# A kernel of two transformer layers whose Fourier stage is computed over half of the frequencies, two groups at a time

## The chip, the cores and the metric

The kernel runs on one core of a Trainium2 chip. The metric is the device time of one execution in microseconds (us): the median over runs, 1680.04 us for the kernel before (three runs, 1679.36 to 1681.76). All inputs, weights included, lie in the chip's main memory at the start.

## The reference, cut to what matters

The model has two layers. Each has a token mixer and a channel mixer, both with a modulated norm ahead and a residual add behind, on 256 tokens of context and 256 tokens of x, each 1024 wide. Half of the mixer's width (512) goes through a gated linear attention, the other half through a Fourier mix:

```
def fourier_mix(u):
    B, L, _ = u.shape                                   # L = 256
    ug = u.reshape(B, L, FNET_GROUPS, FNET_GROUP_DIM)   # 4 groups of 128
    y = jnp.fft.fftn(ug, axes=(1, 3), norm='ortho').real
    return y.reshape(B, L, FNET_WIDTH)

mx = jnp.concatenate([fourier_mix(ux), yx], axis=-1) @ w_out   # yx: the attention
x = x + g1x * mx
hx = modulate(rmsnorm(x, norm_ffn_w[l]), sh2x, sc2x)
x = x + g2x * channel_mixer(hx, ...)     # layer 0: SwiGLU; layer 1: 8 experts
```

The context takes the same path in layer 0; the last layer computes only x behind its attention. The gates and shifts (g1x, sh2x, ...) are sums of a vector of 1024 with a matrix `w_mod` of 1024 x 6144 for each layer.

## The kernel before, in words

Every product of fp32 matrices is made of three matmuls in a rounded format: each operand x is split into a high part (ACT copies x into the rounded type, line 145 for weights) and a low part (DVE subtracts the high part from x, line 149), and `mm3` (lines 155 to 158) adds high x high (L156), low x high (L157) and high x low (L158) in one PSUM bank. A split of one operand is thus one ACT and one DVE instruction, and the first matmul waits for ACT, the one that takes the low part for DVE.

The Fourier mix (`fourier`, lines 729 to 758) takes one sequence of 256 tokens and one group of 128 channels at a time: eight pairs of both in layer 0, four in layer 1. Stage 1 transforms along the tokens: two `mm3` (two blocks of 128 tokens) with the split table `dl_h`, `dl_l` of 512 columns, 256 cosines and 256 sines; ACT and DVE split the result into `vh` and `vl` (L752, L753). Stage 2 (`along_group`) transforms along the channels of a group: two `mm3` with the tables `dd_h`, `dd_l` on the cosine half and the sine half of `vh`, `vl`, both added in one bank of 256 columns; ACT and DVE split this into a block of `cat` (L740, L741), which is an operand of the output projection. Stage 2 of a group is issued behind stage 1 of the next.

Around it: the attention (`gla`), of which pieces are pulled in between groups; `w_out` (the output projection, lines 812 to 860), two halves of 512 columns for each sequence, with its weights split in L145 and L149 and the results multiplied and added to the residual by DVE (L829, L830); and the modulation sums of `mod_chunk`: DVE multiplies and adds blocks of `w_mod` (L422, 128x512 each), PE sums the 128 partitions of the result by four matmuls of one column (L432), DVE copies the sums (L434) into `modc`, and `ac` (L356) is made of `modc`. The norm ahead of the channel mixer (`Norms`, `h_steps`) squares the residual on ACT (L934), takes the root (L195), scales on DVE (L947, `xn`), transposes `xn` on PE (L290, 16 for a sequence), and makes from each transposed block, by `ac` and `modc`, the value (L303 on ACT or L301 on DVE), its high part (L304 or L300, ACT) and its low part (L305, DVE) in `hbk`. The feed-forward of layer 0 begins with three products on the context's tokens alone (72 matmuls of 256 columns), then takes the transposes and blocks of x, then three products on x alone; from there it takes all 512 tokens at once.

The order of the instructions on each engine is fixed when the program is built: a scheduler places each instruction by its priority (its place in the program text, changed by `high_priority` and by `later` for L422) and by its own estimate of when its inputs are ready. So a change of durations in one place can move other instructions past each other.

## Time and profile before

| | |
|---|---|
| median of three runs | 1680.04 us |
| the profiled execution, its own time | 1679.86 us |
| its span, first to last instruction | 1678.1 us |
| PE (TensorE matmuls) busy | 97% of the span |
| DVE (VectorE) busy | 63% |
| ACT (ScalarE) busy | 43% |
| mean granted TensorE clock | 0.993 of full speed |
| Fourier stage of layer 0 | about 179 to 216 us |
| output projection of layer 0 | about 213 to 262 us |
| feed-forward of layer 0 | from 263 us |
| Fourier stage of layer 1 | about 745 to 763 us |
| experts | about 800 to 1660 us |

A matmul is shown with the time that it takes through the array, and matmuls overlap; what one costs is the distance from its start to the next one's. An idle time of PE stands in square brackets, with what ended it. In the rows by windows the columns are the window, its length, then busy us of PE, weight loads, DVE, ACT and POOL with the number of instructions, the granted clock, the busy share of the DMA engines and the GB/s that they moved. In the rows by lines the columns behind the bar are the busy time in us, the mean ns of one, and the idle time ahead of them with what ended it.

### The profile page before, as it was taken

What the parts mean: (1) busy time and instruction counts of PE and PEld (TensorE: products, weight loads), DVE (VectorE), ACT (ScalarE), POOL (GpSimd) and SP (SyncE); (2) the same over time, 40 slices, a digit from 0 to 9 for tenths busy, and PEclk for the clock granted to TensorE, in tenths of its full rate; (3) what the DMA queues carried; (4) which work ended last, traced back from release to release, by engine and by line L of the source; (5) the groups of instructions that cost most, each with busy time, mean ns of one, the idle gap of its engine ahead of it and who ended that gap; (6) DMA issues with size and microseconds to landing.
All of it is one profiled execution on the core that took longest, in us unless ns stands there. A gap on an engine that the chain in (4) does not pass through costs nothing.

```text
span 1678.1 us, 21544 instructions
## 1 busy us (share of the span) xinstructions
PE 1620.3 (97%) x8134; PEld 1168.2 (70%) x8134; DVE 1049.4 (63%) x1318; ACT 726.0 (43%) x890; POOL 26.9 (2%) x51
## 2 busy tenths in 40 slices
PE   7999999999999999999999999999999999999995
PEld 3777888788888888788787347874468844578532
DVE  3798898778667657756996217862078820588322
ACT  3733445322222246554775126751167611567201
POOL 1000000000000000000000000000000000000000
PEclk9999999999999999999999999999999999999998
DMA  9524375556666534545898999999999999999995
GB/s 362 164 85 131 113 250 167 153 180 184 189 198 191 155 126 137 177 164 196 323 359 314 400 408 413 407 411 407 408 411 411 409 390 408 410 414 406 387 405 199
DMA packets 186795, 479.01 MB, mean 285 GB/s; under 512 B 11761, under 2 KB 65201, under 8 KB 172081
## 3 DMA queue, kind: packets, MB, share of 16 engines
q1 hardware_dynamic: 185040, 473.80, 76.4%
q10 hardware_dynamic: 1074, 2.72, 0.5%
q8 instruction: 68, 1.11, 0.3%
q0 software_dynamic: 560, 0.94, 0.2%
q14 instruction: 53, 0.43, 0.1%
HBM read 476.37 MB, written 1.05 MB: 285 GB/s over the span
## 4 chain that ended last, share of the span: by engine, by line
PE 87%; DVE 5%; DMA 3%; ACT 2%; issue 1%; SPq 0%; POOL 0%; DVEq 0%; ACTq 0%; POOLq 0%
PE h L1582 11%; PE mm L156 9%; PE mm L157 9%; PE mm L158 8%; PE h L1591 6%; PE h L1594 6%; PE h L1590 6%; PE y L156 5%; PE y L157 5%; PE y L158 5%; PE y L1614 4%; DMA rr<-moe_w 2%; PE sc L589 1%; PE sc L1561 1%; PE sc L1383 1%
## 5 line engine op out<-in xcount | busy, mean ns | idle before, releaser
L145 ACT ACTIVATE hi<-raw 128x1024 fp32r<-128x1024 f32 x127 | 134.5, 1060 | 309.2 <-PE mm L157 94.2
L177 DVE TENSOR_TENSOR rb<-raw,rb 128x2048 fp32r<-128x2048 f32 x73 | 167.1, 2290 | 79.8 <-ACT rb L177 59.6
L149 DVE TENSOR_TENSOR lo<-raw,hi 128x1024 fp32r<-128x1024 f32 x127 | 155.3, 1224 | 87.6 <-ACT hi L145 86.3
L422 DVE SCALAR_TENSOR_TENSOR rr<-rr,cs,rr 128x512 f32<-128x512 f32 x256 | 181.7, 748 | 10.9 <-DMA rr<-b_mod 5.3
L1591 PE MATMUL h<-rb,hg 128*128 128x512 f32 x448 | 177.2, 395 | 4.1 <-DVE rb L177 4.0
L156 PE MATMUL mm<-hbk,hi 128*128 128x512 f32 (+1 forms) x456 | 166.5, 366 | 0.9 <-DVE tm L829 0.7
L157 PE MATMUL mm<-hbk,hi 128*128 128x512 f32 (+1 forms) x456 | 163.7, 360 | 0.5 <-DVE hbk L305 0.5
L158 PE MATMUL mm<-hbk,lo 128*128 128x512 f32 (+1 forms) x456 | 163.7, 359 | 0.0
L177 ACT ACTIVATE rb<-raw 128x2048 fp32r<-128x2048 f32 x73 | 139.9, 1917 | 50.7 <-PE h L1594 31.9
L1582 PE MATMUL h<-raw,hgs 128*64 128x512 f32 (+1 forms) x720 | 143.4, 529 | 0.0
L177 DVE TENSOR_TENSOR sil<-sil,h 128x512 f32<-128x512 f32 (+1 forms) x44 | 29.2, 663 | 165.7 <-PE h L1582 148.5
L1590 PE MATMUL h<-rb,hg 128*128 128x512 f32 x288 | 109.1, 399 | 1.6 <-ACT rb L177 1.6
L1582 PEld LDWEIGHTS h<-raw,hgs 128*64 128x64 f32 x720 | 51.6, 137 | 77.5 <-issue 68.9
L1591 PEld LDWEIGHTS h<-rb,hg 128*128 128x128 f32 x448 | 85.2, 190 | 26.1 <-DVE rb L177 6.3
L177 DVE TENSOR_TENSOR rb<-raw,part 128x2048 fp32r<-128x2048 f32 x42 | 96.1, 2288 | 10.5 <-PE h L1591 4.6
L156 PEld LDWEIGHTS mm<-hbk,hi 128*128 128x128 f32 x456 | 85.8, 189 | 16.3 <-issue 2.4
L177 DVE TENSOR_TENSOR rb<-rr,rb 128x2048 fp32r<-128x2048 f32 x35 | 80.0, 2288 | 27.2 <-ACT rb L177 23.7
L177 ACT ACTIVATE part<-raw 128x2048 fp32r<-128x2048 f32 x42 | 80.4, 1914 | 36.4 <-DMA raw<-moe_w 17.0
L157 PEld LDWEIGHTS mm<-hbk,hi 128*128 128x128 f32 x456 | 85.9, 189 | 14.1 <-issue 1.0
L158 PEld LDWEIGHTS mm<-hbk,lo 128*128 128x128 f32 x456 | 85.9, 189 | 13.0
L1594 PE MATMUL h<-rb,hg 128*128 128x512 f32 x288 | 88.5, 393 | 2.5 <-DVE hg L177 2.5
L157 PE MATMUL y<-rb,ht 128*128 128x512 f32 x224 | 87.6, 391 | 0.0
(381 smaller groups left out, 2984.6 us busy)
## 6 DMA issues: line engine op xcount, KB each, us to landing
raw<-moe_w SPq DMA_DIRECT2D x212, 1024.0 KB
rr<-moe_w SPq DMA_DIRECT2D x110, 1024.0 KB
rr<-w_mod SPq DMA_DIRECT2D x80, 512.0 KB
raw<-ffn_w SPq DMA_DIRECT2D x72, 512.0 KB
raw<-w_in SPq DMA_DIRECT2D x32, 512.0 KB
raw<-w_out SPq DMA_DIRECT2D x23, 512.0 KB
raw<-moe_w SPq DMA_DIRECT2D x12, 512.0 KB
rb<-w_mod SPq DMA_DIRECT2D x5, 1024.0 KB
```

Of the source, the lines that this page charges most:

```text
L145: ins = nc.scalar.activation(hi, raw, AF.Copy).ins
L149: nc.vector.tensor_tensor(lo, raw, hi.bitcast(F32), op=OP.subtract)
L156: nc.tensor.matmul(ps, lh, rh, start=start, stop=False)
L157: nc.tensor.matmul(ps, lh, rl, start=False, stop=False)
L158: nc.tensor.matmul(ps, ll, rh, start=False, stop=stop)
L177: r = getattr(self.engine, name)(*args, **kw)
L422: nc.vector.scalar_tensor_tensor(accs[x], rv[:, k, :], cs[:, x * 8 + kb:x * 8 + kb + 1], accs[x], op0=OP.mult, op1=OP.add)
L1582: nc.tensor.matmul(H[i][0][x * 64:x * 64 + 64, :n], HG[e][:, k0 + j, :], hi[:, j, x * n:(x + 1) * n], start=(k0 + j == 0), stop=(k0 + j == 7))
L1590: nc.tensor.matmul(H[i][b], hgh[:, kb, :], hi[:, j, bc], start=(kb == 0), stop=False)
L1591: nc.tensor.matmul(H[i][b], hgh[:, kb, :], lo[:, j, bc], start=False, stop=False)
L1594: nc.tensor.matmul(H[i][b], hgl[:, kb, :], hi[:, j, bc], start=False, stop=(kb == 7))
L1614: nc.tensor.matmul(Y[e][0][hh * 64:hh * 64 + 64], ht[:, j0 + j, half], hi[:, j, xc], start=on, stop=off)
```

## The change

The token transform of a real sequence has a symmetry: cosines of frequency l and 256 - l are the same, sines differ in sign. So the table keeps 128 cosine columns (frequencies 0 to 127), the cosine of frequency 128 in the unused place of sine 0, and 127 sine columns. Stage 1 takes 256 columns for a group instead of 512, and the bank of 512 holds two groups, so that one ACT and one DVE instruction split both; the tiles of the table (`dlr`, `dl_h`, `dl_l`) and its load are half as wide. In stage 2 the cosine part and the sine part of two groups are products of 256 columns of their own (no sum of both on PE), the frequency 128 is a `mm3` of four columns into another bank (`mid`), ACT copies the sine part to SBUF (`sn`), DVE adds both parts for the frequencies 1 to 127 and subtracts them, written backwards, for 255 to 129, ACT copies two single columns for 0 and 128, and from this `y`, in SBUF now, ACT and DVE make the high and low part of each group, as before from PSUM. Stage 2 of two groups is issued behind stage 1 of the next two.

```diff
-    dl = np.concatenate([np.cos(ang), np.sin(ang)], 1).reshape(2, 128, 512).transpose(1, 0, 2)
+    dl = np.concatenate([np.cos(ang[:, :128]), np.cos(ang[:, 128:129]), np.sin(ang[:, 1:128])], 1)
+    dl = dl.reshape(2, 128, 256).transpose(1, 0, 2)
...
-            def along_group(s, g, vh, vl):
-                p2 = psp.tile([128, 512], F32, name="mm", tag="mm", bufs=4)[:, :256]
+            def along_groups(s, g, vh, vl):
+                bank_ = psp.tile([128, 512], F32, name="mm", tag="mm", bufs=4)
+                p2 = bank_.rearrange("p (c g l) -> p c g l", c=2, g=2)
                 for r in range(2):
-                    rr = slice(r * 256, (r + 1) * 256)
-                    mm3(p2, dd_h[:, r, :], dd_l[:, r, :], vh[:, rr], vl[:, rr], r == 0, r == 1)
-                cb = cat(g)
+                    mm3(p2[:, r].rearrange("p g l -> p (g l)"), dd_h[:, r, :], dd_l[:, r, :],
+                        vh[:, r].rearrange("p g l -> p (g l)"), vl[:, r].rearrange("p g l -> p (g l)"), True, True)
+
+                mid = bank()[:, 0:4].rearrange("p (g l) -> p g l", g=2)
+                mm3(mid, dd_h[:, 0, :], dd_l[:, 0, :], vh[:, 1, :, 0:2], vl[:, 1, :, 0:2], True, True)
+                sn = temp()[:, 0:256].rearrange("p (g l) -> p g l", g=2)
+                nc.scalar.activation(sn.rearrange("p g l -> p (g l)"), bank_[:, 256:512], AF.Copy)
+                y = temp().rearrange("p (g l) -> p g l", g=2)
+                nc.vector.tensor_tensor(y[:, :, 1:128], p2[:, 0, :, 1:128], sn[:, :, 1:128], op=OP.add)
...
+                nc.vector.tensor_tensor(back, p2[:, 0, :, 1:128], sn[:, :, 1:128], op=OP.subtract)
+                nc.scalar.activation(y[:, :, 0:1], p2[:, 0, :, 0:1], AF.Copy)
+                nc.scalar.activation(y[:, :, 128:129], mid[:, :, 0:1], AF.Copy)
                 o0 = s * 256 - coff
-                hi, lo = cb[:, 0, o0:o0 + 256], cb[:, 1, o0:o0 + 256]
-                nc.scalar.activation(hi, p2, AF.Copy)
-                nc.vector.tensor_tensor(lo, p2, hi.bitcast(F32), op=OP.subtract)
+                for k in range(2):
+                    cb = cat(g + k)
+                    hi, lo = cb[:, 0, o0:o0 + 256], cb[:, 1, o0:o0 + 256]
+                    nc.scalar.activation(hi, y[:, k], AF.Copy)
+                    nc.vector.tensor_tensor(lo, y[:, k], hi.bitcast(F32), op=OP.subtract)
 
             for s in seqs:
-                for g in range(4):
-                    vh = mx.tile([128, 512], F32R, name="vh", tag="vh", bufs=2)
-                    vl = mx.tile([128, 512], F32R, name="vl", tag="vl", bufs=2)
+                for g in (0, 2):
+                    vh = mx.tile([128, 2, 2, 128], F32R, name="vh", tag="vh", bufs=2)
+                    vl = mx.tile([128, 2, 2, 128], F32R, name="vl", tag="vl", bufs=2)
                     ps = psp.tile([128, 512], F32, name="mm", tag="mm", bufs=4)
-                    for t in range(2):
-                        uc = slice(g * 128, (g + 1) * 128)
-                        mm3(ps, uh[:, 2 * (s - sb) + t, uc], ul[:, 2 * (s - sb) + t, uc], dl_h[:, t, :], dl_l[:, t, :],
-                            t == 0, t == 1)
-                    nc.scalar.activation(vh, ps, AF.Copy)
-                    nc.vector.tensor_tensor(vl, ps, vh.bitcast(F32), op=OP.subtract)
+                    for k in range(2):
+                        uc = slice((g + k) * 128, (g + k + 1) * 128)
+                        for t in range(2):
+                            mm3(ps[:, k * 256:(k + 1) * 256], uh[:, 2 * (s - sb) + t, uc], ul[:, 2 * (s - sb) + t, uc],
+                                dl_h[:, t, :], dl_l[:, t, :], t == 0, t == 1)
+                        if k == 0:
+                            yield
+                    pv = ps.rearrange("p (g c l) -> p c g l", g=2, c=2)
+                    nc.scalar.activation(vh, pv, AF.Copy)
+                    nc.vector.tensor_tensor(vl, pv, vh.bitcast(F32), op=OP.subtract)
                     if pend:
-                        along_group(*pend)
+                        along_groups(*pend)
                     pend = (s, g, vh, vl)
                     yield
-            along_group(*pend)
+            along_groups(*pend)
...
```

The lines of the changed kernel are numbered two higher than before up to the Fourier stage, and 21 higher behind it (L290 is now L292, L305 is L307, L422 is L424, L432 is L434, L434 is L436, L829 is L850, L830 is L851, L947 is L968). The scheduler moves instructions at the following places; the rows are the engine's own order, and behind a name stands its number in this program (the numbers of both programs differ by a few for the same tile).

On PE, at the end of layer 0's output projection, before: `mm_2070` and `mm_2071` are results of the third of its four parts, `xn_2064` is the context's scaled residual, and `mm_2334` the first product of the feed-forward.

```order
L156 MATMUL mm_2070<-hi_2149,rb1_1547 128x512
L157 MATMUL mm_2070<-lo_2150,rb1_1547 128x512
L158 MATMUL mm_2070<-hi_2149,rb1_1547 128x512
L290 MATMUL sc_2072<-sqc_79,xn_2064 128x128 [waits DVE_49,PE_49]
L290 MATMUL sc_2103<-sqc_79,xn_2064 128x128 [waits PE_49]
L290 MATMUL sc_2134<-sqc_79,xn_2064 128x128 [waits PE_49]
L156 MATMUL mm_2071<-hi_2149,rb0_1541 128x512
L157 MATMUL mm_2071<-lo_2150,rb0_1541 128x512
...
L158 MATMUL mm_2211<-hi_2268,rb2_1553 128x512
L156 MATMUL mm_2334<-hbk_1870,hi_2330 128x256 [waits DVE_49,Activation_49]
```

The same place now; `sc_1830` and `sc_1836` are the partition sums of the last piece of the shift and scale ahead of the feed-forward, `mm_2206` is the last part's result and `mm_2330` the first product of the feed-forward.

```order
L159 MATMUL mm_2206<-lo_2265,rb1_1536 128x512
L434 MATMUL sc_1830<-sqc_79,rr2_66 128x1 [waits DMAHW2_49,DVE_49,PE_49]
L434 MATMUL sc_1830<-sqc_79,rr2_66 128x1 x3
L160 MATMUL mm_2206<-hi_2264,rb1_1536 128x512
...
L160 MATMUL mm_2207<-hi_2264,rb1_1536 128x512
L434 MATMUL sc_1836<-sqc_79,rr2_66 128x1 [waits DMAHW4_49,DVE_49,PE_49]
L434 MATMUL sc_1836<-sqc_79,rr2_66 128x1 x3
L292 MATMUL sc_2068<-sqc_79,xn_2060 128x128 [waits PE_49]
L292 MATMUL sc_2068<-sqc_79,xn_2061 128x128
...
L292 MATMUL sc_2161<-sqc_79,xn_2061 128x128
L158 MATMUL mm_2330<-hbk_1866,hi_2326 128x256 [waits DVE_49,Activation_49]
L159 MATMUL mm_2330<-hbk_1866,hi_2326 128x256 [waits DVE_49]
```

The 16 transposes of the context, which stood among the products of the third part, and the two sets of partition sums, which stood there or just ahead, are now behind the products of the last part; the first product of the feed-forward follows the transposes at once and each of its triples waits for ACT and DVE.

On DVE the copies of these sums (L434, now L436) and the scale `ac` of the context's norm (L356, now L358) go with them: they stood ahead of the low parts (L149) of the last seven weight units up to the third of the feed-forward, and stand behind all seven now. The first low parts of the context's norm (L305, now L307) stand behind the last residual adds (L830, now L851).

On DVE, between the scaling of x (`xn`) and the first block of x in the feed-forward (`hbk_1870` on `h32_2426`), before:

```order
L947 TENSOR_SCALAR xn_2322<-resid2_1866,rsy_2289 128x1024 [waits DVE_49]
L256 TENSOR_TENSOR rsy_2302<-rsy_2302,rsv_2303 128x1 [waits DVE_49]
L422 SCALAR_TENSOR_TENSOR rr2_66<-rr1_65,cs_91,rr2_66 128x512
L947 TENSOR_SCALAR xn_2323<-resid3_1868,rsy_2302 128x1024 [waits DVE_49]
L422 SCALAR_TENSOR_TENSOR rr2_66<-rr1_65,cs_91,rr2_66 128x512
L422 SCALAR_TENSOR_TENSOR rr2_66<-rr1_65,cs_91,rr2_66 128x512 [waits DVE_49]
L422 SCALAR_TENSOR_TENSOR rr2_66<-rr0_64,cs_91,rr2_66 128x512 [waits DMAHW4_49,DVE_49]
L422 SCALAR_TENSOR_TENSOR rr2_66<-rr0_64,cs_91,rr2_66 128x512 [waits DVE_49] x2
L305 TENSOR_TENSOR hbk_1870<-h32_2426,hbk_1870 128x256 [waits Activation_49]
```

And now (`hbk_1866` on `h32_2422`):

```order
L968 TENSOR_SCALAR xn_2319<-resid3_1864,rsy_2298 128x1024 [waits DVE_49]
L424 SCALAR_TENSOR_TENSOR rr2_66<-rr0_64,cs_91,rr2_66 128x512
L424 SCALAR_TENSOR_TENSOR rr2_66<-rr0_64,cs_91,rr2_66 128x512 [waits DVE_49] x2
L424 SCALAR_TENSOR_TENSOR rr2_66<-rr1_65,cs_91,rr2_66 128x512 [waits DMAHW3_49,DVE_49]
L424 SCALAR_TENSOR_TENSOR rr2_66<-rr1_65,cs_91,rr2_66 128x512 [waits DVE_49] x3
L424 SCALAR_TENSOR_TENSOR rr2_66<-rr0_64,cs_91,rr2_66 128x512 [waits DMAHW6_49,DVE_49]
L424 SCALAR_TENSOR_TENSOR rr2_66<-rr0_64,cs_91,rr2_66 128x512 [waits DVE_49] x3
L307 TENSOR_TENSOR hbk_1866<-h32_2422,hbk_1866 128x256 [waits Activation_49]
```

Between the second `xn` and the first low part stood five modulation sums (the last row stands for two), and eleven stand there now.

On PE, at the end of layer 1's Fourier stage, before: `mm_6243` is stage 2 of the last group, `mm_6271` a result of the output projection.

```order
L157 MATMUL mm_6233<-vl_6203,dd_h_85 128x256
L158 MATMUL mm_6233<-vh_6202,dd_l_86 128x256
L156 MATMUL mm_6243<-vh_6222,dd_h_85 128x256 [waits Activation_49]
L156 MATMUL mm_6271<-hi_6275,hbk_6187 128x512 [waits DVE_49]
L157 MATMUL mm_6271<-lo_6276,hbk_6187 128x512
L158 MATMUL mm_6271<-hi_6275,hbk_6187 128x512
L156 MATMUL mm_6271<-hi_6275,hbk_6187 128x512
L157 MATMUL mm_6271<-lo_6276,hbk_6187 128x512
L158 MATMUL mm_6271<-hi_6275,hbk_6187 128x512
L157 MATMUL mm_6243<-vl_6223,dd_h_85 128x256 [waits DVE_49]
```

And now, with `mm_6223` as stage 2 of the last two groups, `sc_6230` their product of four columns and `mm_6265`, `mm_6266` results of the output projection:

```order
L158 MATMUL mm_6223<-vh_6183,dd_h_85 128x256 [waits Activation_49]
L158 MATMUL sc_6230<-vh_6183,dd_h_85 128x4
L159 MATMUL mm_6223<-vl_6184,dd_h_85 128x256 [waits DVE_49]
L160 MATMUL mm_6223<-vh_6183,dd_l_86 128x256
L158 MATMUL mm_6223<-vh_6183,dd_h_85 128x256
L159 MATMUL mm_6223<-vl_6184,dd_h_85 128x256
L160 MATMUL mm_6223<-vh_6183,dd_l_86 128x256
L159 MATMUL sc_6230<-vl_6184,dd_h_85 128x4
L160 MATMUL sc_6230<-vh_6183,dd_l_86 128x4
L158 MATMUL mm_6265<-hi_6269,hbk_6218 128x512 [waits PE_49,Activation_49]
L159 MATMUL mm_6265<-lo_6270,hbk_6218 128x512
```

Six products of the output projection stood inside the last stage 2, and ran while DVE made `vl`; the last stage 2 now stands in one piece ahead of them.

## Rows read from the trace of the kernel before

**Rows 1.** Waits of PE, 170 to 330 us: total us, times, longest.

```profile
PE mm L156 <- DVE tm L829: 0.7, 1, 0.7
PE mm L157 <- DVE hbk L305: 0.5, 1, 0.5
```

**Rows 2.** Windows: PE, PEld, DVE, ACT, POOL busy us; clock, DMA share, GB/s.

```profile
240.00:260.00 20.00, 20.00 (x101) 16.73 (x100) 19.23 (x40) 14.90 (x30) 0.53 (x1) 1.00 0.60 185
260.00:280.00 20.00, 18.66 (x146) 17.56 (x145) 18.84 (x39) 10.63 (x25) 0.00 (x0) 1.00 0.64 185
```

**Rows 3.** Timeline of PE, layer 0's Fourier stage: start, us, line.

```profile
179.62 0.39 PE L158 MATMUL mm<-dl_h,ul 128*128 128x512 f32 x1
179.85 0.39 PE L156 MATMUL mm<-dl_h,uh 128*128 128x512 f32 x1
...
183.74 0.28 PE L157 MATMUL mm<-vl,dd_h 128*128 128x256 f32 x1
183.86 0.28 PE L158 MATMUL mm<-vh,dd_l 128*128 128x256 f32 x1
...
184.34 1.84 PE L432 MATMUL sc<-sqc,rr 128*128 128x1 f32 x16
```

**Rows 4.** Timeline of PE, layer 0's output projection to FFN.

```profile
212.96 0.40 PE L156 MATMUL mm<-hi,rb 128*128 128x512 f32 x1
...
241.61 0.95 PE L432 MATMUL sc<-sqc,rr 128*128 128x1 f32 x8
...
262.80 0.35 PE L156 MATMUL mm<-hbk,hi 128*128 128x256 f32 x1 [0.75 <-DVE tm L829]
...
271.50 1.91 PE L290 MATMUL y<-sqc,xn 128*128 128x128 f32 x16
...
282.96 0.40 PE L156 MATMUL mm<-hbk,hi 128*128 128x512 f32 x1
```

**Rows 5.** Lines of DVE, 179.28 to 274.14 us: busy us, mean ns, idle.

```profile
L422 DVE SCALAR_TENSOR_TENSOR rr<-rr,cs,rr 128x512 f32<-128x512 f32 x51 | 35.8, 746 | 0.0
L753 DVE TENSOR_TENSOR vl<-mm,vh 128x512 fp32r<-128x512 f32 x8 | 5.5, 686 | 3.8 <-ACT vh L752 3.8
L741 DVE TENSOR_TENSOR rb<-mm,rb 128x256 fp32r<-128x256 f32 x8 | 3.3, 415 | 0.0
L726 DVE TENSOR_TENSOR rb<-e,rb 128x256 fp32r<-128x256 f32 x8 | 3.0, 420 | 0.3 <-ACT rb L725 0.2
```

**Rows 6.** Lines of ACT, 179 to 216 us, same columns.

```profile
L752 ACT ACTIVATE vh<-mm 128x512 fp32r<-128x512 f32 x8 | 4.8, 594 | 5.7 <-PE mm L158 5.7
L740 ACT ACTIVATE rb<-mm 128x256 fp32r<-128x256 f32 x8 | 3.0, 381 | 2.9 <-PE mm L158 2.4
L725 ACT ACTIVATE rb<-e 128x256 fp32r<-128x256 f32 x8 | 3.0, 409 | 0.6 <-DVE rb L726 0.6
```

**Rows 7.** Timeline of ACT at context normalisation and rsqrt.

```profile
255.08 1.02 ACT L303 ACTIVATE h<-sc,modc,ac 128x256 f32<-128x256 f32 x2
255.98 0.73 ACT L304 ACTIVATE hbk<-h 128x256 fp32r<-128x256 f32 x2
256.60 0.64 ACT L934 ACTIVATE sq<-resid 128x512 f32<-128x512 f32 x1
...
265.86 0.29 ACT L195 ACTIVATE rsy<-ss 128x1 f32<-128x1 f32 x1
...
267.34 1.28 ACT L188 ACT_TABLE_LOAD   x1
```

**Rows 8.** Timeline of DVE before the X half of the FFN.

```profile
270.83 3.39 DVE L422 SCALAR_TENSOR_TENSOR rr<-rr,cs,rr 128x512 f32<-128x512 f32 x5
```

**Rows 9.** Timeline of PE, end of layer 1's Fourier stage.

```profile
759.45 0.38 PE L156 MATMUL mm<-vh,dd_h 128*128 128x256 f32 x1 [0.74 <-ACT vh L752]
```

**Rows 10.** Windows of the expert stage, columns of rows 2.

```profile
860.00:920.00 60.00, 60.00 (x288) 48.42 (x289) 44.65 (x28) 37.63 (x31) 0.00 (x0) 1.00 0.93 339
920.00:1000.00 80.00, 77.61 (x398) 33.19 (x396) 13.32 (x17) 13.43 (x22) 0.00 (x0) 1.00 1.02 401
```

More of the change, by code (lines that the diff above doesn't have):

```diff
@@ L214, in hybrid_kernel @@
     masks = cA.tile([128, 8, 128], mybir.dt.uint8, name="masks")[:, 0:7]
-    dl_h = cA.tile([128, 2, 512], F32R, name="dl_h")
-    dl_l = cA.tile([128, 2, 512], F32R, name="dl_l")
+    dl_h = cA.tile([128, 2, 256], F32R, name="dl_h")
+    dl_l = cA.tile([128, 2, 256], F32R, name="dl_l")
     dd_h = cA.tile([128, 2, 128], F32R, name="dd_h")
@@ L730, in fourier @@
             pend = None
-            def along_group(s, g, vh, vl):
-                p2 = psp.tile([128, 512], F32, name="mm", tag="mm", bufs=4)[:, :256]
+            def along_groups(s, g, vh, vl):
+                bank_ = psp.tile([128, 512], F32, name="mm", tag="mm", bufs=4)
+                p2 = bank_.rearrange("p (c g l) -> p c g l", c=2, g=2)
                 for r in range(2):
-                    rr = slice(r * 256, (r + 1) * 256)
-                    mm3(p2, dd_h[:, r, :], dd_l[:, r, :], vh[:, rr], vl[:, rr], r == 0, r == 1)
-                cb = cat(g)
-                o0 = s * 256 - coff
-                hi, lo = cb[:, 0, o0:o0 + 256], cb[:, 1, o0:o0 + 256]
-                nc.scalar.activation(hi, p2, AF.Copy)
-                nc.vector.tensor_tensor(lo, p2, hi.bitcast(F32), op=OP.subtract)
+                    mm3(p2[:, r].rearrange("p g l -> p (g l)"), dd_h[:, r, :], dd_l[:, r, :],
[6 more added lines that the diff above has]
+                nc.vector.tensor_tensor(y[:, :, 1:128], p2[:, 0, :, 1:128], sn[:, :, 1:128], op=OP.add)
+                back = y[:, 0, 255:256]
+                back = bass.AP(tensor=back.tensor, offset=back.offset, ap=[list(back.ap[0]), [256, 2], [-1, 127]])
+                nc.vector.tensor_tensor(back, p2[:, 0, :, 1:128], sn[:, :, 1:128], op=OP.subtract)
+                nc.scalar.activation(y[:, :, 0:1], p2[:, 0, :, 0:1], AF.Copy)
+                nc.scalar.activation(y[:, :, 128:129], mid[:, :, 0:1], AF.Copy)
+                o0 = s * 256 - coff
+                for k in range(2):
[3 more added lines that the diff above has]
+                    nc.vector.tensor_tensor(lo, y[:, k], hi.bitcast(F32), op=OP.subtract)
@@ L868, in cat0 @@
         return cats[kb]
-    dlr = mx0.tile([128, 2, 512], F32, name="dlr", tag="ul")
+    dlr = mx0.tile([128, 2, 256], F32, name="dlr", tag="ul")
     mkr = mx0.tile([128, 9, 128], I32, name="mkr", tag="uh")
```

## The prediction

> **What bounds the kernel now.** I read the waits of PE first. From 170 to 330 us, where layer 0's Fourier stage, output projection and first feed-forward products lie, PE waits for other engines only 1.2 us in all, for one DVE product and one DVE low part [rows 1]. Read alone, that says that PE bounds the stage and that each matmul taken away is time gained. The busy times by window say something else: from 240 to 280 us DVE is busy 19.23 and 18.84 of each 20 us beside PE's 20.00 and 18.66 [rows 2]. Both are full. What fills DVE is the modulation sums: 51 of L422 take 35.8 us between the start of the Fourier stage and the first low part of x in the feed-forward, and none of them ever made DVE idle [rows 5]. They have low priority, so DVE looks busy with work that could be done later, but only where the order lets it. The reader should see that a shorter PE stage here runs into a DVE queue that is no shorter.
>
> Whatever shift remains reaches the end. From 860 us on the DMA engines are busy 0.93, from 920 on 1.02 of the time [rows 10], but while they are below full the loads start when earlier weights are used up, so an earlier start of the experts is an earlier start of the saturated stretch too. I carry shifts through one to one.
>
> **The change, part by part: PE.** Successive starts stand 0.23 us apart for 512 columns and 0.12 us for 256 [rows 3]. For two groups stage 1 had 12 matmuls of 512 columns and has 12 of 256: 12 x 0.11 = 1.3 us saved. Stage 2 had 12 of 256 and has 6: 0.7 us saved. Three matmuls of four columns are added. Before has none; the nearest is the sum over partitions with one column, 16 in 1.84 us, so about 0.10 us each (the last one's tail left out) [rows 3]: 0.3 us. Bounds are 0 (fully beside others) and 0.36 (a 256-column one each). I take 0.3 and get 1.7 us for two groups: 7.0 us for the four pairs of layer 0, 3.5 us for the two of layer 1, 10.4 us in all.
>
> The Trainium skill ("TensorE: Matmul & The Clock Gate", Back-to-back issue gap) gives a start-to-start floor of about 25 ns for so few columns; by it the three would cost 0.08 us and the whole gain be about 11.8 us. The trace disagrees: each of these matmuls brings its own 128 columns of weights, and 0.10 us is measured.
>
> **ACT and DVE.** For two groups ACT had two `vh` of 594 ns and two high parts of 381 ns, 1.95 us [rows 6]. It now has one of 594, the sine copy (256 columns from PSUM, 381), two high parts from SBUF (409, the row of L725, which has that form) and two copies of two columns. For those the nearest row is a 128x1 activation of 0.29 us [rows 7]; bounds 0.1 and 0.38. Sum 2.4 us. DVE had two of 686 and two of 415, 2.2 us [rows 5]; it has one of 686, an add and a subtract of 254 columns (415 each, one operand in PSUM; backwards writing is not in the trace, I take the same, between 415 and the 686 of twice the columns) and two low parts from SBUF (420, L726's row): 2.35 us. So neither becomes shorter, and the path behind the last stage 2 becomes longer: before, one high and one low part (0.8 us); now sine copy, add, subtract, two tiny copies, high, low, in turn on ACT and DVE: 0.38 + 2 x 0.42 + 2 x 0.29 + 0.41 + 0.42 = 2.6 us to the first operand of `w_out`. PSUM banks come free only behind the tiny copies.
>
> **Layer 0.** In the order shown, the output projection waits for a bank until the tiny copies are done, and for `vl` of the last pair (686 behind 594 ns). Following the instructions from the Fourier stage on with these durations, PE loses about 3.5 of its 7.0 us, and is through the projection, the partition sums and the 16 transposes of the context at about 258.4 us (between 255, no wait, and 262, all lost), where it now starts its first feed-forward product at 262.80 [rows 4].
>
> But the context's norm, which ran inside the projection, now begins there: the column sums, their DVE copies and `ac` come last. ACT then has six L303 (two from 255.08 to 255.98), six L304 (two from 255.98 to 256.60), two L300 (about as L303), two squares of 0.64 and the small roots (0.29, four) and a table load of 1.28 us [rows 7]: 2.7 + 1.9 + 0.9 + 1.3 + 1.0 + 1.3 = 9.1 us, to about 267. The first 24 feed-forward matmuls fit between the blocks, the other 48 follow at 0.12: 5.8 us, so the context's part ends near 273.3, where it ended at 271.50 [rows 4].
>
> DVE is stricter. From the copy of the last sums (about 256.6) to x's first low part it must do two gate products and two residual adds left over, eight low parts, two blocks of L301, both `xn`, some twelve small steps and 16 modulation sums, eleven of them in one piece behind the second `xn` where five stood. Five took 3.39 us [rows 8], 0.68 each: 16 are 10.9 us; the rest, at the lengths that rows 5 give for such shapes, about 9.1 us. 256.6 + 20.0 = 276.6 us without any idling. It was 274.2 (270.83 + 3.39) [rows 8]. So x's half starts 2.4 us later, and everything behind it: 282.96 [rows 4] becomes about 285.4. Layer 0: **+2.4 us**, from -7.0 (nothing of this binds) to +6 (a load late besides).
>
> **Layer 1.** Here no such norm follows at once. Of 3.5 us the chain behind the last stage 2 takes some back: before, PE waited 0.74 us for `vh` [rows 9] and ran six `w_out` products while DVE made `vl`; now the last stage 2 waits for `vl` in full (up to 1.5 us) and `w_out` for the first high part (about 1.1 us), against the 0.74 that goes. I get **-1.5 us**, between -3.5 (covered by other products) and +0.5 (both waits at the full 2.6).
>
> **The start.** The table's load and split are half as long, about 0.6 us of ACT, as a 512-column copy [rows 6]. On the path it is worth 0 to 0.6: **-0.3 us**.
>
> Sum: 2.4 - 1.5 - 0.3 = +0.6 us on the profiled execution's 1679.86, which is 0.2 below the median of 1680.04: 1680.6 for a median forecast of about 1680.7. A measurement of this kernel tells 0.2%, about 3.4 us, from no change. So: no change, by two effects that cancel.
>
> **Rivals.** *PE bounds everything:* all 10.4 us pass, 1669.5. For it: 1.2 us of waits [rows 1]. Against: DVE's 38 of 40 us [rows 2], and more work on the path to `w_out`. 6%.
>
> *Half of it passes:* DVE's sums have slack of many us later, and if PE gets through the context without being held (the norm's ACT chain overlapping better than 9.1 us), layer 0 comes out at about -1.5 and layer 1 at -3: with the start 1675. 14%.
>
> *A modulation sum waits for its load:* three sums now stand between the blocks of the context's norm and eleven ahead of x's first block, each in DVE's strict order, so a `w_mod` block that has not landed stops the norm itself. The projection runs 3.5 us earlier, and so asks earlier. A block of 512 KB takes 2.8 us at the 185 GB/s of that stretch [rows 2]; it decides as soon as one load is later than the sum's place in the queue. +0.6 + 2.8 = 3.4, and two of them 6.2: 1683.5 to 1686. Against it: no sum waited before [rows 5]. 20%.
>
> *The clock falls:* with PE held between 258 and 267 us it does a third of its usual work. The granted clock is 1.00, that is 2.4 GHz, through all of these windows [rows 2], with hardly any waits. If it fell to 1.2 GHz, the 48 products behind would start 0.23 apart, not 0.12: +5.5, 1686. 4%. The Trainium skill's same page (Why this matters for your kernels) advises against idle gaps of PE between bursts for this reason; no gap of this size is in these rows.
>
> That the change does not do what it says can be left out: the order shows the 256-column matmuls.
>
> **How the numbers follow.** Forecast 56%, within about 3 us of 1680.7 mostly: 50 of it within 0.2%, 4 above, 2 below. The two faster rivals hold 20%, the two slower ones 24%. Faster 0.22, within 0.2% 0.50, slower 0.28. The range leaves out the full gain, part of the half gain and the far end of the slow ones: 1675 to 1686. The forecast's own range is 1677.5 to 1683.5.
>
> **What would show it.** In the changed profile: starts 0.12 apart in stage 1, three four-column matmuls of about 0.1 us; the first `w_out` product of layer 0 some 5 us before 212.96; waits of PE for the tiny copies and `vl`; the first context product near 259 instead of 262.80 and triples with gaps up to 267; eleven sums in one piece, x's first low part near 276.6, and the first 512-column feed-forward product near 285.4. In layer 1 `w_out` about 1.5 us earlier. I would be wrong if that 512-column product came before 281 (PE was the bound) or after 288 (a load or the clock), or if layer 1 lost time.

## The result, and the profile after

The changed kernel took 1689.48 us (median of five runs, 1688.37 to 1690.1) where the kernel before took 1679.36 beside it: a ratio of 1.0058 [1.0043, 1.0073], slower by 10 us. The forecast was 1680.7, and its range ended at 1686. The span grew from 1678.1 to 1687.9 us and the mean granted clock fell from 0.993 to 0.984. That is no chance of the profiled run: all five timed runs of the changed kernel have 0.984 to 0.986, and the runs of the kernel before beside the experiments below 0.989 to 0.995. An estimate from these means: 0.015 of 1689 us is 25 us of full-clock work lost, 0.0075 of 1679 before is 13; the difference of 12 is as large as the loss.

Where the 9.8 us lie is read from three marks on PE in both traces (the first Fourier matmul, the first 512-column feed-forward product, and the product that waits 0.64 us for the router's `oh`):

| stretch | before | after | difference | forecast |
|---|---|---|---|---|
| start to Fourier, layer 0 | 179.07 | 179.57 | +0.5 | -0.3 |
| Fourier to 512-column product | 103.89 | 113.09 | +9.2 | +2.4 |
| to the router's product (layer 1 inside) | 510.62 | 510.81 | +0.2 | -1.5 |
| to the end | 884.5 | 884.4 | -0.1 | 0 |

The +0.5 holds a stretch at half clock that the kernel before has too, longer here (6.8 against 3.4 us); in e4 below, where this code is that of before, it was 6.8 too. Nearly all of the rest is layer 0. PE's waits there, 170 to 330 us, answer to [rows 1]:

```profile
PE mm L158 <- ACT hbk L306: 3.2, 3, 1.5
PE mm L158 <- ACT e L751: 2.5, 1, 2.5
PE mm L159 <- DVE hbk L307: 0.6, 2, 0.3
```

These waits are new, the 2.5 for the last of the tiny copies and 3.8 in the context's norm; together they are less than the loss. PE's timeline there, in the kernel after (start us, duration, [idle before it, and what ended it]), answers to [rows 3, 4]:

```profile
203.74 0.28 PE L160 MATMUL mm<-dl_h,ul 128*128 128x256 f32 x1
203.86 0.28 PE L158 MATMUL mm<-dl_h,uh 128*128 128x256 f32 x1
...
207.92 0.50 PE L158 MATMUL mm<-hi,rb 128*128 128x512 f32 x1 [2.47 <-ACT e L751]
...
211.01 0.63 PE L158 MATMUL mm<-hi,rb 128*128 128x512 f32 x1
211.44 0.63 PE L159 MATMUL mm<-lo,rb 128*128 128x512 f32 x1
...
216.20 1.05 PE L434 MATMUL sc<-sqc,rr 128*128 128x1 f32 x8
...
217.89 0.95 PE L434 MATMUL sc<-sqc,rr 128*128 128x1 f32 x8
218.70 0.25 PE L158 MATMUL sc<-vh,dd_h 128*128 128x4 f32 x1
218.81 0.25 PE L159 MATMUL sc<-vl,dd_h 128*128 128x4 f32 x1
...
220.25 0.63 PE L158 MATMUL mm<-hi,rb 128*128 128x512 f32 x1
220.68 0.63 PE L159 MATMUL mm<-lo,rb 128*128 128x512 f32 x1
...
266.15 0.39 PE L158 MATMUL mm<-hbk,hi 128*128 128x256 f32 x1 [1.49 <-ACT hbk L306]
...
281.81 1.91 PE L292 MATMUL y<-sqc,xn 128*128 128x128 f32 x16
...
292.66 0.40 PE L158 MATMUL mm<-hbk,hi 128*128 128x512 f32 x1
```

ACT's timeline has the sine copy and the two tiny copies, for which [rows 6, 7] gave the nearest rows:

```profile
205.52 0.37 ACT L745 ACTIVATE e<-mm 128x256 f32<-128x256 f32 x1
206.14 0.17 ACT L752 ACTIVATE e<-sc 128x2 f32<-128x2 f32 x1 [0.25 <-DVE rb L728]
206.81 0.72 ACT L727 ACTIVATE rb<-e 128x256 fp32r<-128x256 f32 x2 [0.49 <-DVE e L718]
...
207.70 0.16 ACT L751 ACTIVATE e<-mm 128x2 f32<-128x2 f32 x1
```

The matmuls that were to become shorter did: stage 1 starts 0.12 us apart, the four-column ones 0.11, and some only 0.03 (764.85 to 764.88). The reader should compare rows of one shape: 512-column products that start 0.23 apart before start 0.43 apart at 211 and again at 220. Windows over these stretches (PE, PEld, DVE, ACT, POOL busy us; granted clock, DMA share, GB/s) say why:

```profile
209.00:212.00 3.00, 3.00 (x11) 2.52 (x11) 1.79 (x7) 0.45 (x2) 0.00 (x0) 0.50 0.00 0
215.00:219.00 4.00, 4.00 (x28) 3.42 (x26) 3.22 (x6) 1.06 (x1) 0.63 (x2) 1.00 0.53 159
...
220.00:225.00 5.00, 5.00 (x13) 3.85 (x13) 1.95 (x3) 2.30 (x6) 1.40 (x2) 0.50 0.48 151
...
267.00:277.00 10.00, 8.03 (x32) 6.97 (x33) 9.82 (x28) 6.74 (x18) 0.00 (x0) 0.50 0.17 54
```

The clock is at 0.50, its 1.2 GHz level, in three stretches of layer 0. By windows of one us each they are 208.8-212.2, 219.0-225.9 and 266.8-277.1; the first two alone take 5.1 us of full-clock work away. The second comes while PE is never idle, behind sixteen one-column (as the trace counts them) and six four-column matmuls. Windows of 20 us, the answer to [rows 2], dilute it: the third stretch is a 0.74 here.

```profile
260.00:280.00 20.00, 15.85 (x88) 13.76 (x87) 18.92 (x45) 10.63 (x26) 0.87 (x2) 0.74 0.46 135
```

DVE's timeline, from the copy of the last sums to x's first low part, answers to [rows 8]:

```profile
263.80 0.15 DVE L436 COPY modc<-sc 128x4 f32<-128x4 f32 x1
...
275.63 7.37 DVE L424 SCALAR_TENSOR_TENSOR rr<-rr,cs,rr 128x512 f32<-128x512 f32 x11
283.80 0.76 DVE L307 TENSOR_TENSOR hbk<-h,hbk 128x256 fp32r<-128x256 f32 x2 [0.80 <-ACT hbk L306]
```

From copy to low part are 20.0 us, and 8.86 more to the 512-column product: the forecast had 20.0 and 8.8. But the copy stands at 263.80, not 256.6. That 7.2 us is the miss.

Layer 1, the answer to [rows 9]:

```profile
764.15 0.39 PE L159 MATMUL mm<-vl,dd_h 128*128 128x256 f32 x1 [0.49 <-DVE vl L774]
...
766.68 0.39 PE L159 MATMUL mm<-vl,dd_h 128*128 128x256 f32 x1 [1.32 <-DVE vl L774]
...
768.41 0.68 PE L158 MATMUL mm<-hi,hbk 128*128 128x512 f32 x1 [0.74 <-ACT hbk L757]
```

Behind these waits the clock is at 0.50 from 768.6 to 772.0, worth 1.7 us.

### The profile page after: what moved, and what is told of

The parts are those of the page before. It is cut to its first block, busy times and chain, and to the rows that moved or that the text cites. A ratio compares the mean times of both kernels' runs of the same rounds, so it can differ in the third digit from the quotient of the medians.

```text
span 1687.9 us, 21517 instructions
## 1 busy us (share of the span) xinstructions
PE 1622.7 (96%) x8116; PEld 1171.6 (69%) x8116; DVE 1048.7 (62%) x1324; ACT 724.7 (43%) x902; POOL 26.8 (2%) x51
## 4 chain that ended last, share of the span: by engine, by line
PE 86%; DMA 4%; DVE 4%; ACT 3%; issue 1%; SPq 0%; POOL 0%; DVEq 0%; ACTq 0%; POOLq 0%
PE h L1603 11%; PE mm L158 9%; PE mm L159 9%; PE mm L160 9%; PE h L1612 6%; PE h L1615 6%; PE h L1611 6%; PE y L158 5%; PE y L159 5%; PE y L160 5%; DMA rr<-moe_w 3%; PE y L1635 3%; PE sc L591 1%; PE sc L1582 1%; PE sc L1404 1%
## 5 line engine op out<-in xcount | busy, mean ns | idle before, releaser
L424 DVE SCALAR_TENSOR_TENSOR rr<-rr,cs,rr 128x512 f32<-128x512 f32 x256 | 181.5, 747 | 11.4 <-DMA rr<-b_mod 5.7
L158 PE MATMUL mm<-hbk,hi 128*128 128x512 f32 (+1 forms) x456 | 168.0, 370 | 3.3 <-ACT hbk L306 3.2
L159 PE MATMUL mm<-hbk,hi 128*128 128x512 f32 (+1 forms) x456 | 165.9, 364 | 0.6 <-DVE hbk L307 0.6
```

Source lines behind the costliest of these rows:

```text
L158: nc.tensor.matmul(ps, lh, rh, start=start, stop=False)
L159: nc.tensor.matmul(ps, lh, rl, start=False, stop=False)
L424: nc.vector.scalar_tensor_tensor(accs[x], rv[:, k, :], cs[:, x * 8 + kb:x * 8 + kb + 1], accs[x], op0=OP.mult, op1=OP.add)
```

## The experiments

Two theories. A: the loss is TensorE's clock, which falls behind the new waits and behind the new run of few-column matmuls. B: the loss is the context's norm, which the change moves behind the output projection, and the clock only accompanies it. The expectations of e1 to e4 use the letters for the question of their own run (in e1 the late norm is A); the text between them uses them as here. "FFN mark" is the first 512-column product (282.96 before, 292.66 after).

**e1: the sums early (kernel after).** The norm's inputs lose their lateness, so that it runs inside the projection again.

```diff
-                    with later(LATER):
+                    with later(0 if l == 0 and col >= 3 * D and col < 5 * D else LATER):
```

> The changed kernel, but the modulation sums for the shift and scale ahead of layer 0's feed-forward keep their own place in the order (they are no longer put off), so that the context's norm lies inside the output projection again. Theory A (the late norm is the greater part of the loss, and its gaps let the clock fall): the first 512-column product of the feed-forward, at 292.66 us in the changed kernel and 282.96 before, comes at 281 to 285; time 1679 to 1682. Rival B (the longer chain behind the last stage 2 and more DVE work are the loss, the norm is incidental): it stays above 289; time above 1686.

Measured: 1681.15 us, ratio to before 1.0015 [1.0006, 1.0025], FFN mark 285.86. Most of the loss goes, as B says; but so do stretches at half clock, and others come (208-214, 266-269, 761-767). It does not tell A from B.

**e2: wide columns (kernel after).** The partition sums over 128 columns, the frequency-128 product over 256.

```diff
-                    nc.tensor.matmul(ps[:, j:j + 1], accs[x][:, j * 128:(j + 1) * 128], ones[:, 0:1],
+                    nc.tensor.matmul(ps[:, j * 128:(j + 1) * 128], accs[x][:, j * 128:(j + 1) * 128], ones,
...
-                mm3(mid, dd_h[:, 0, :], dd_l[:, 0, :], vh[:, 1, :, 0:2], vl[:, 1, :, 0:2], True, True)
+                mm3(mid.rearrange("p g l -> p (g l)"), dd_h[:, 0, :], dd_l[:, 0, :],
+                    vh[:, 1].rearrange("p g l -> p (g l)"), vl[:, 1].rearrange("p g l -> p (g l)"), True, True)
```

> The changed kernel, but the partition sums write 128 columns instead of one, and the product for frequency 128 takes 256 columns instead of four; a matmul's weights take about as long as these columns, so PE's time hardly changes. Theory A: a run of matmuls with few columns (16 and 6 of them, from 216.2 to 219.6 us) lets the granted clock fall to 0.50 from 219.0 to 225.9; with more columns that fall is gone and 2 to 4 us come back (1685.5 to 1687.5), while the late norm and its fall remain. Rival B (the fall at 219 follows from the wait of 2.5 us before it): the clock falls there as before, time 1688.5 to 1690.

Measured: 1680.27, ratio 1.0011 [1.0001, 1.002], below both ranges of its expectation; FFN mark 284.93. No stretch at half clock lies between 132 and 261 us; one from 261.5 to 268.4 does, at a wait of 4.6 us. But the order changed as well: the context's transposes moved into the projection (251.5). One clean reading stays: layer 1, without a fall near 768, takes 508.92 us from mark to mark, 1.7 below before.

**e3: the late norm alone (kernel before).**

```diff
-                nc.vector.tensor_copy(cols_out[x], ps[:, 0:4])
+                with later(3000 if l == 0 and col == 4 * D + 512 else 0):
+                    nc.vector.tensor_copy(cols_out[x], ps[:, 0:4])
```

> The kernel before, with the old Fourier stage, but the copies of the last partition sums ahead of layer 0's feed-forward put off on DVE, so that the context's norm comes behind the output projection as in the changed kernel. Theory A: this alone costs 4 to 8 us (1683.5 to 1687.5), the clock falls while PE is held between the norm's blocks. Rival B: under 2 us, since PE has other products meanwhile.

Measured: 1693.08, ratio 1.0075 [1.0058, 1.0092], 14 us slower, where 4 to 8 were expected; FFN mark 296.47. The dose was larger than the change's own. Its one long wait, from the timeline of PE:

```profile
272.49 1.94 PE L290 MATMUL sc<-sqc,xn 128*128 128x128 f32 x8 [10.06 <-DVE modc L435]
```

The clock stood at 0.50 from 264.8 to 278.4. A late norm costs by itself; how much the change's own costs this does not say.

**e4: wide sums (kernel before)**, the first edit of e2 alone.

> The kernel before with partition sums that write 128 columns instead of one. Theory A: before has no fall of the clock near its partition sums, so nothing changes: 1678 to 1681. Rival B (wider columns help anywhere): faster by 2 us or more.

Measured: 1678.11, ratio 0.9995 [0.9985, 1.0004]: no change, as expected. Wide sums gain nothing in a kernel without half clock at its narrow ones.

**f1 and f2: matmuls of no use as filling (kernel after)**; f2 adds two more ahead of each block of the first context product.

```diff
             along_groups(*pend)
+            warm = psp.tile([128, 512], F32, name="sc", tag="sc", bufs=4)
+            wv = pend[2].rearrange("p c g l -> p (c g l)")
+            for _ in range(11 if first else 5):
+                nc.tensor.matmul(warm, dd_h[:, 0, :], wv, start=True, stop=True)
```

> The kernel after, with 512-column matmuls of no use (their result is never read) put in behind the last Fourier stages: 11 in layer 0, 5 in layer 1. They keep TensorE busy where it waited 2.47 us for a 4-column copy at 207.92, and in layer 1 1.32 and 0.74 us ahead of the fall of the clock at 768.8; by the after trace's 0.22 us each at full clock they cost up to 2.4 us in layer 0 and 1.1 in layer 1, less what TensorE waited there anyhow. Theory A (the loss is the clock, halved after TensorE's short waits): the stretch at half clock at 208.9-212.1 is gone and so the one at 768.8-772.0, and the time is 3 to 5 us below the kernel after, 1684.5 to 1686.5. Inside A, the stretch at half clock at 219.0-225.9 goes too if it was an after-effect of the wait at 207.92, and stays if the run of one-column and four-column matmuls ahead of it makes it. Theory B (the loss is the later norm and its copies, the clock only a passenger): TensorE's extra work costs what it costs, 1689.5 to 1691.

> The kernel before's successor (after) with the same idle matmuls of no use as in f1, and two more ahead of each of the eight blocks of the first context product of layer 0's FFN, where TensorE waited 1.49, 0.33, 0.72, 0.28 and 0.97 us for hbk between 266.15 and 273.58 and ran at half clock to 277.0. Theory A (the clock after short waits): that stretch is gone as well, the first 512-column product of the FFN falls to 285-288 from 292.66, the time to 1680-1684. Theory B (the later norm itself): the extra 16 matmuls come on top or lie inside the waits, 1689 to 1692.

Measured: f1 1685.64, ratio 1.0045 [1.0027, 1.0063]; f2 1689.87, 1.0063 [1.0045, 1.008]. In layer 0 both missed their places. In f1 the eleven ran from 220.01, behind the few-column matmuls, and PE's wait of 2.47 us stayed; so did the stretches at 209 and 219 (the latter half as long), while those at 266 and 768 are gone. In f2 the sixteen waited for ACT's `h` themselves, 4.0 us in all, and the clock was at 0.50 from 269 to 276 all the same. So in layer 0 A's first half, that filling the gap keeps the clock up, was not put to the test, and f1's time inside A's range is no proof of it. In layer 1 the five did stand in the gap, in f1 and in f2; PE's timeline of f1:

```profile
763.01 1.40 PE L783 MATMUL sc<-vh,dd_h 128*128 128x512 f32 x5
```

The wait of 1.32 us is gone, those of 0.49 and 0.76 remain, and neither profile has half clock behind them. Of the seven other profiles with the change in layer 1 and its three waits, six have it there (the kernel after, e1, g1, g2, g3, h2; not e2). That speaks for A's first half; two cases are few.

**f3, f4, h3: bursts in the kernel before**, in a stretch where PE never waits and the clock is 1.00. Each burst is 32 matmuls of 1 column (f3), 32 of 128 (f4) or 11 of 1 (h3), ahead of each of 14 groups. In the trace each of these matmuls, whose operands are plain fp32, stands twice, so that a burst is 64, 64 or 22 in a row; those of f1, in the rounded format, stand once.

```diff
             for n in ("ffn_w1", "ffn_w3"):
+                if gi:
+                    warm = up_bank()
+                    for _ in range(32):
+                        nc.tensor.matmul(warm[:, 0:1], ones, ones[:, 0:1], start=True, stop=True)
```

> The kernel before, with 32 matmuls of one column each (128x128 ones as weights, one bank, never read) ahead of each of 14 groups of layer 0's FFN, where TensorE never waits and the clock stands at 1.00. By the 0.10 us that a one-column matmul took in the before trace, 32 take 3.2 us, 14 times that is 45 us. If a run of few-column matmuls makes the clock fall though TensorE is busy (the second half of theory A), rows behind the bursts show 0.43 us per 512-column matmul for some us, the profile shows stretches at 0.50 there, and the time is 1679 + 45 + 14 x about 2 to 4 us = 1750 to 1780. If only idle time makes it fall, no stretch at 0.50 shows there, and the time is 1715 to 1728.

> As f3, each of the 32 matmuls with 128 columns in place of one: the same count, the same weights, the same bank. By the 0.10 to 0.11 us from start to start of 128-column matmuls with their own weights in the before trace, 14 x 3.3 = 47 us. In both theories the clock stays at 1.00 and the time is 1715 to 1728; f3 less f4 is then what few columns alone cost: 0 to 3 us if only idle time counts, 28 us or more if few columns do.

> As f3 with 11 one-column matmuls in each of the 28 bursts in place of 32: the order there puts two bursts behind each other, 22 in a row, as many as the one- and four-column matmuls that stood at 216.2-219.7 in the kernel after. By 0.14 us each (9.02 for 64 in f3) 28 x 11 x 0.14 = 43 us if the clock falls within or behind each pair, by 0.11 (full clock) 34. If so short a run is enough to make the clock fall: stretches at half clock in 400-600, and 1720 to 1750. If it needs the longer run: clock 1.00 there, 1711 to 1716, and the stretch at 219-226 of the kernel after needs the wait at 207.9 as its cause besides.

Measured: f3 1842.75 us, f4 1778.36, h3 1724.6. (The sums of f3 and f4 had counted each matmul once; the 28 bursts and pairs in the expectation of h3 are 14 bursts whose matmuls stand twice.) PE in windows (busy us; clock, DMA share, GB/s), f3 and then f4:

```profile
500.00:520.00 20.00, 20.00 (x94) 0.74 0.19 60
520.00:540.00 20.00, 20.00 (x100) 0.74 0.32 102
```

```profile
500.00:520.00 20.00, 20.00 (x131) 1.00 0.50 158
520.00:540.00 20.00, 20.00 (x132) 1.00 0.19 57
```

PE is busy 20.00 of 20 us in both. The first burst of f3, then of f4:

```profile
405.73 9.02 PE L1043 MATMUL mm<-sqc 128*128 128x1 f32 x64
...
415.18 0.63 PE L157 MATMUL mm<-hbk,hi 128*128 128x512 f32 x1
415.61 0.63 PE L158 MATMUL mm<-hbk,lo 128*128 128x512 f32 x1
```

```profile
406.27 7.31 PE L1043 MATMUL mm<-sqc 128*128 128x128 f32 x64
...
413.64 0.40 PE L157 MATMUL mm<-hbk,hi 128*128 128x512 f32 x1
413.88 0.39 PE L158 MATMUL mm<-hbk,lo 128*128 128x512 f32 x1
```

All 14 bursts of f3 have a stretch at 0.50, in and behind them, and none of f4's. Few columns alone, without idle time, lower the clock; the difference is 64.4 us, 4.6 for each burst. In h3, with 22 in a row, as many few-column matmuls as the kernel after has at 216-220 (there with three wide products among them), 8 of the 14 bursts have half clock in or behind them. The first of them:

```profile
407.63 2.51 PE L1043 MATMUL mm<-sqc 128*128 128x1 f32 x22
410.01 0.48 PE L156 MATMUL mm<-hbk,hi 128*128 128x512 f32 x1
...
410.78 0.40 PE L156 MATMUL mm<-hbk,hi 128*128 128x512 f32 x1
411.00 0.60 PE L157 MATMUL mm<-hbk,hi 128*128 128x512 f32 x1
411.40 0.63 PE L158 MATMUL mm<-hbk,lo 128*128 128x512 f32 x1
```

Such a run can lower the clock by itself, and does not always.

**g1: the frequency-128 product alone over 256 columns (kernel after)**, the second edit of e2. On PE the order is that of the kernel after, except that the context's transposes come one group of three products earlier.

> The kernel after, with the frequency-128 product alone over 256 columns in place of 4 (its result is read in the same columns); the partition sums stay at one column. On TensorE the order stays the same up to the end of layer 0's w_out, so the stretch at half clock at 219.0-225.9, behind sixteen one-column and six 4-column matmuls, can be looked at by itself; the context norm's transposes come one group of three products earlier. By 0.12 us from start to start of 256-column matmuls against 0.11 of 4-column ones, the twelve in layer 0 and six in layer 1 cost 0.2 us. Theory A (few columns make the clock fall): that stretch is shorter or gone and the time is 1 to 4 us below the kernel after, 1685.5 to 1688.5. Theory B (the stretch is an after-effect of the 2.47 us wait at 207.9, or has nothing to do with columns): it stays, and the time is 1689 to 1690.

Measured: 1681.93, ratio 1.0018 [1.0009, 1.0028], 7.6 us below the kernel after: more than the 1 to 4 that A gave. Rows of PE, then of DVE (lines behind the edit are numbered one higher here):

```profile
207.12 0.50 PE L158 MATMUL mm<-hi,rb 128*128 128x512 f32 x1 [1.12 <-ACT e L752]
...
216.33 0.36 PE L158 MATMUL sc<-vh,dd_h 128*128 128x256 f32 x1
...
217.36 0.40 PE L158 MATMUL mm<-hi,rb 128*128 128x512 f32 x1
217.59 0.39 PE L159 MATMUL mm<-lo,rb 128*128 128x512 f32 x1
...
285.46 0.40 PE L158 MATMUL mm<-hbk,hi 128*128 128x512 f32 x1
```

```profile
255.77 0.16 DVE L436 COPY modc<-sc 128x4 f32<-128x4 f32 x1 [0.56 <-PE sc L434]
...
269.33 7.37 DVE L424 SCALAR_TENSOR_TENSOR rr<-rr,cs,rr 128x512 f32<-128x512 f32 x11
276.62 0.75 DVE L307 TENSOR_TENSOR hbk<-h,hbk 128x256 fp32r<-128x256 f32 x2
```

No stretch at half clock at 209 or 219 is left (one from 263.4 to 270.3, inside the norm, and one in layer 1, 761.8 to 765.2, are), and the steps of the forecast are all there: copy at 255.8 (256.6 forecast), low part at 276.62 (276.6), 512-column product at 285.46 (285.4). The norm is as late as in the kernel after, behind the projection, so B as the whole cause falls; net of what the shorter matmuls save, it costs the 2.5 us by which this mark is behind the kernel before, 1.9 of them behind the first Fourier matmul. Not one thing changed, though: ACT's order moved a little, and the wait at 207 shrank from 2.47 to 0.35 and 1.12.

**g2: the change in layer 1 alone (kernel before)**, with the half table read out of the whole one (`fourier_half` is `fourier` of the kernel after).

```diff
+        if not first:
+            for x in (dl_h, dl_l):
+                nc.gpsimd.tensor_copy(x[:, :, 256:257], x[:, :, 128:129].bitcast(F32))
-        for _ in fourier():
+        for _ in (fourier() if first else fourier_half()):
```

> The change in layer 1 alone: layer 0 keeps the whole transforms of the kernel before, and in layer 1 the half table is read out of the whole one (whose column of zero sines is overwritten, on GpSimd, by the 128th cosine). The step of the prediction for layer 1 (-1.5 us) is tested by itself. If it holds and the clock stays up in layer 1: 1676.5 to 1677.7 against 1678.6 for the kernel before, ratio 0.9988 to 0.9995; if the clock falls near 768 as it did in the kernel after (1.7 us): 1678.5 to 1679.5; if layer 0's loss is not in the clock and the norm but in something general of the change: above 1680.

Measured: 1679.35, ratio 1.0001 [0.9992, 1.0009]: no change, as expected for a clock that falls; its profile, of the slowest of the twelve runs, has 0.50 from 757.6 to 764.4.

**g3, h2: e1 and e2 together; h1: the same remedies in the kernel before.**

> The kernel after with both remedies: the partition sums of layer 0's columns 3D to 5D without their 250 of lateness (as in e1), these sums over 128 columns and the frequency-128 product over 256 (as in e2). TensorE's order has the context norm's transposes inside w_out and no run of few-column matmuls. If the loss of the kernel after is the clock and the late norm, both are gone: with no stretch at half clock besides that at 127-134, 1675 to 1678; with one more of about 8 us (as e1 and e2 each had behind a wait in w_out), 1679 to 1682. If something else of the change costs the time, 1684 or more.

> g3 once more, beside the two others on one chip, for its lead over the kernel before. If the lead is real: 1675.5 to 1677.5, ratio 0.998 to 0.999. If it was the draw of one call: 1678 to 1680.

> The kernel before with the remedies of g3 that it can take: the same partition sums without their 250 of lateness, over 128 columns; the whole transforms stay. It tells whether g3's gain over the kernel before (1676.4 against 1678.8) is the change's or the remedies'. If the change's: the same as the kernel before within its interval or slower (the kernel before had neither a late norm nor a run of few-column matmuls there), 1678 to 1681, and g3 stays 2 us or more ahead. If the remedies': 1675.5 to 1677.

Measured: g3 1676.36, ratio 0.9982 [0.9973, 0.9991]; h2 1676.26, 0.9983 [0.9973, 0.9992]; h1 1680.47, 1.0007 [0.9997, 1.0016]. With both remedies the changed kernel beats the kernel before by 0.17%, twice, and the remedies without the change gain nothing. In g3 layer 0 has no stretch at half clock from 133 us on and the FFN mark is at 281.61, 1.4 ahead of before; layer 1 still has one (756.8-760.2).

## Why the prediction was wrong, point by point

- **PE's saving** (0.23 to 0.12 us a start, 0.10 for a four-column matmul): right in size (0.12; 0.11, where some follow in 0.03). The row behind the 0.10 was read as 16 matmuls; they are eight, each of which stands twice.
- **ACT and DVE behind the last stage 2:** right in kind. The tiny copies took 0.16 and 0.17 us, not 0.29, but the last of them stood behind the attention's high parts (L727) and DVE's work ahead of these: `w_out` waited 2.47 us, and began at 207.92, 5.0 ahead of 212.96 as forecast.
- **Layer 0, PE "is through ... at about 258.4 us":** this step failed. Its sum counts every matmul at the distance of the full clock and so puts a fall of the clock at nothing. The transposes ended at 264.7 and the last copy of the sums came at 263.80 instead of 256.6. Two stretches at half clock ahead of it take 5.1 of these 7.2 us, and the kernel started this stage 0.8 later than forecast; the other 1.3 were not traced to one cause. The 512-column product came at 292.66, behind the 288 that the prediction gave as a sign of "a load or the clock".
- **Layer 0, DVE's 20.0 us and what follows:** right to 0.1 us in the kernel after, and in g1, where the two stretches are missing, the absolute times too; but in part by luck. Of the 20.0 us of the kernel after DVE stood idle for 0.80, waiting for ACT and by it for PE's transposes at 281.81, so PE under the third stretch ended it and not DVE. In g1 the copy came 0.8 us earlier than forecast and the way from it to the low part took 20.85. The late norm is real, and layer 0 comes out near the forecast without the two stretches (+2.5 in g1, 1.9 of them behind the first Fourier matmul; +2.4 forecast).
- **Layer 1, -1.5:** the chain was right (-1.7 in e2, where the clock held); with the clock's fall it is +0.2 in the kernel after, and nothing over all runs in g2.
- **A shift reaches the end one to one:** right (884.5 and 884.4 us behind the router's product), with two stretches of 3.4 us at half clock in each before the last ones, at other places.
- **"The clock falls", 4%, 1686:** the mechanism was named and priced as the least likely, and put in one place, the gap at 258-267, where it cost about 0.8 us, the wait of DVE at 283.80. It was ruled out with "no gap of this size is in these rows" and a clock of 1.00 over windows of 20 us. The trace of before already showed the case; its timeline of PE has

```profile
128.49 3.54 PE L428 MATMUL sc<-rr,sqc 128*128 128x512 f32 x4 [3.42 <-issue]
```

and by windows of 1 us the clock is at 0.50 there, from 128.3 to 131.7. This row was not read. The prediction itself had worked out a hand-over wait on the way to `w_out` of 2.6 us, and did not ask what the clock does behind it.

The Trainium skill ("TensorE: Matmul & The Clock Gate", Why this matters for your kernels) advises against idle gaps of PE between bursts. The trace agrees in kind: half clock follows the gap of 2.47 us at 207.92, though the gaps that the page warns of are longer; the measurement decides. That section does not speak of the second stretch, at 219, which came without a gap; that is f3's finding.

- **Other rivals:** the two faster ones are out, since the time rose, and no modulation sum was late by a load in the stretch from 263.80 to 283.80, which took the forecast 20.0 us.

What stays open: whether the stretch at 219 in the kernel after is the few-column run's alone (h3: in 8 of 14 cases) or needed the wait at 207.9 besides. Since g1 changed both, it doesn't part them.

## What to carry to other kernels

Making matmuls shorter on a PE that was full made waits here, and each wait or run of narrow matmuls can bring several us of half clock behind it, in one execution and not in the next: read the granted clock by windows of one us around every wait of more than a us, in the trace before the change as well. Where a value for a few columns is needed, computing 128 or 256 columns cost next to nothing on PE here (0.11 us each, with 128 columns in f4 as with one in h3), and in f4 the clock stayed up. When a change moves work out of an order that was well filled, set the order right again before judging the change: here the same arithmetic was 0.6% slower and, with the small edits of e1 and e2, 0.17% faster.

## What the runs showed of the hardware

- PE at 20.00 of 20 us busy had its clock at 0.74 with one-column matmuls among its products and at 1.00 with 128-column ones in their place, count and weights alike (f3, f4).
- 64 matmuls of one column took 9.02 us where 64 of 128 columns took 7.31: the narrow ones were the slower; the clock stood at 0.50 from 410.8 on.
- Whether a short run lowers the clock varies from one case to the next (h3: 8 of 14; its two timed runs lie 12 us apart, 1718.64 and 1730.57).
- The same holds for a wait. All 16 profiles have one of 2.5 us at the start of the experts, with the same products behind it; in 12 the clock is at 0.50 behind it (in the kernel after from 809.5 to 812.9), in four, the kernel before among them, it stays at 1.00. PE's timeline of before, then of after:

```profile
799.09 0.73 PE L1594 MATMUL h<-rb,hg 128*128 128x512 f32 x2 [2.53 <-DVE hg L177]
```

```profile
808.98 0.79 PE L1615 MATMUL h<-rb,hg 128*128 128x512 f32 x2 [2.54 <-DVE hg L179]
```

So one stretch at half clock in one profile proves little by itself; the mean clock of all timed runs, and a run repeated, prove more.
